# Second attention: turned 16-bit probability parts used as they are, and values kept as scaled pairs of 16-bit floats

## The chip, the cores and the metric

One core of a Trainium2 chip. The metric is the device time of one execution in microseconds (us). The engines that matter here: TensorE (PE; its weight loads are PEld), VectorE (DVE), ScalarE (ACT), GpSimd (POOL) and the queue of SyncE (SP), which issues the DMAs. Each engine runs its instructions in the order in which they stand on it.

## What is computed

A decoder of two layers over 512 positions of 1024 features. Layer 0 mixes with two block-sparse attentions, layer 1 with a "forgetting" attention (FoX) of 16 heads of 64; each layer ends in a squared-ReLU MLP. The change touches the second attention alone, `fox`:

```
q, k, v, fz = split(rmsnorm(h) @ w_in)
log_f = log_sigmoid(fz + b_forget);  cum = cumsum(log_f)
s = q.k * scale + cum[query] - cum[key];  p = softmax over keys <= query
o = p @ v;   h = h + concat(o) @ w_out
```

## The kernel before

All matrix products are made of pairs: a 32-bit operand is split into a high part (a rounding copy on ScalarE) and a low part (the operand less the high part, a subtraction on VectorE or GpSimd), and `mm3` adds three products, high·high, high·low and low·high. Weights come from DRAM in pieces of at most 128x1024 into a pool `raw` of five buffers; `split` issues the DMA and returns a function `parts`, which makes the pair in a pool `whl` of three. `load_cols` returns these functions and `cols` calls them at once. A string (`FOX_LOW`) says for each piece whether its low part is made by VectorE (D) or GpSimd (P).

`fox` runs as follows. `wv = self.cols(...)` loads and splits the first 272 columns of value and forget weights, in three pieces (3, 3 and 2 of the eight row blocks; 816, 816 and 544 columns). `norm_t` normalises the four row tiles of the residual stream, each in a buffer `xn` of the pool `raw` too: a Square with its sum on ScalarE, a chain of nine one-column operations on VectorE (`inv_rms`), a multiplication with the gain, eight transposes on TensorE, and again a pair, `xhi` (ScalarE) and `xlo` (VectorE). A string then orders the steps:

```
FOX_ORDER = "v0 f k0 k1 p0 k2 v1 p1 k3 p2 o01 k4 v2 p3 k5 p4 k6 v3 p5 k7 p6 o23 p7 o45 o67"
```

`v` are values of four heads (for each of four row tiles 24 matmuls into a PSUM bank `acc`, then a ScalarE copy and a VectorE subtraction into the pair `V[t]`), `f` the forget sums, which go through DRAM as extra rows of keys and queries, `k` queries and keys of two heads, `p` softmax and values of two heads, `o` the output projection.

For one head, `softmax_t` makes scores, exponentials and sums of four query tiles, scales the probabilities by 32768 over the sum and writes them as two 16-bit parts (`HL`: high by ScalarE, low by VectorE and GpSimd). One transposing DMA turns both into `HT`. One head later, `behind` takes them up: `turned` copies the turned high part to a 32-bit tile `PTh` on ScalarE and the turned low part to `PTl` on GpSimd; `pv` multiplies them with the value pair, eight matmuls of 512, 512, 384, 384, 128, 128, 256 and 256 columns; `combine` adds the halves and scales by 1/32768.

The instructions of all steps are put in order by a scheduler that works from its own model of durations, with `prio()` and `high_priority` ahead of the rest. Buffers are taken from their pool in that order: whatever needs a buffer stands behind what frees it.

Of the kernel before, what the change touches and what calls it, by code (L numbers as in the profile page):

```python
# [48 lines left out]
class Trunk:  # L49
# [28 lines left out]
    def split(self, srcs, shape, pool):  # L78


        nc = self.nc
        a, b = shape
        n = a * b
        raw = self.raw.tile([P, W_RAW], F32, tag="raw", name=self.nm("raw"))
        rv = raw[:, :n].rearrange("p (a b) -> p a b", a=a)
        for c0, c1, src in srcs:
            self.last_load = nc.sync.dma_start(rv[:, :, c0:c1], src)

        def parts():
            hl = (pool or self.whl).tile([P, 2, W_RAW], FR, tag="whl", name=self.nm("whl"))  # L90
            nc.scalar.activation(hl[:, 0, :n], raw[:, :n], AF.Copy)  # L91
            eng = nc.gpsimd if self.phase[self.pieces % len(self.phase)] == "P" else nc.vector
            self.pieces += 1
            eng.tensor_tensor(hl[:, 1, :n], raw[:, :n], hl[:, 0, :n].bitcast(F32), op=ALU.subtract)  # L94
            hv = hl[:, :, :n].rearrange("p t (a b) -> p t a b", a=a)
            return [(hv[:, 0, i], hv[:, 1, i]) for i in range(a)]
        return parts
# [310 lines left out]
    def softmax(self, passes, band, gate):  # L408

        nc = self.nc  # L410
        pt = self.pP.tile([P, PTW], F32, tag="P", name=self.nm("P"))
        st = self.sm.tile([P, 3, 4], F32, tag="sst", name=self.nm("sst"))
# [14 lines left out]
    def transpose_p(self, p):  # L427

        nc = self.nc
        hi = self.pPT.tile([P, PTW], FR, tag="PTh", name=self.nm("PTh"))  # L430
        lo = self.pPT.tile([P, PTW], FR, tag="PTl", name=self.nm("PTl"))
        for off, js in BANKS:
# [48 lines left out]
        nc.sync.dma_start_transpose(t, hl.rearrange("p a b -> p (a b)"))  # L481
        return t

    def turned(self, t):


        tv = t.rearrange("p (a b) c -> p a (b c)", a=2)
        hi = self.pPT.tile([P, PTW], FR, tag="PTh", name=self.nm("PTh"))
        lo = self.pPT.tile([P, PTW], FR, tag="PTl", name=self.nm("PTl"))
        with self.tc.issue_after(self.p_act.ins):  # L490
            self.nc.scalar.activation(hi, tv[:, 0], AF.Copy)
        with self.tc.issue_after(self.p_low.ins):
            self.round(lo, tv[:, 1])
        return hi, lo

    def pv(self, po, pt, vs, first, last):
        mm = self.nc.tensor.matmul
        js = [0, 1, 3, 2]
        for i, j in enumerate(js):
            w = S - j * P  # L500
            o = PTOFF[j]
            mm(po[:, j * P:], vs[j], pt[0][:, o:o + w], start=first and i == 0, stop=False)  # L502
            mm(po[:, j * P:], vs[j], pt[1][:, o:o + w], start=False, stop=last and i == 3)  # L503

    def combine(self, po, o, lower, scale=None):

        a, b = (slice(0, HD), slice(HD, P)) if lower else (slice(HD, P), slice(0, HD))
        if scale is None:
            self.nc.scalar.activation(o[a], po[b], AF.Copy)
            self.nc.vector.tensor_tensor(o[a], po[a], o[a], op=ALU.add)  # L510
        else:
            self.nc.scalar.activation(o[a], po[b], AF.Copy, scale=scale)
            self.nc.vector.scalar_tensor_tensor(o[a], po[a], scale, o[a], op0=ALU.mult, op1=ALU.add)

    def split_o(self, o):
        hl = self.pO.tile([P, 2, S], FR, tag="O", name=self.nm("O"))
# [668 lines left out]
    def fox(self, hs):  # L1185
        self.phase, self.pieces = FOX_LOW, 0
        nc, I = self.nc, self.I
        w = I["odd_w_in"][0]
        wo = I["odd_w_out"][0]
        lo, hi = slice(0, HD), slice(HD, P)  # L1190
        with ExitStack() as cx:
            pool = lambda name, bufs: cx.enter_context(self.tc.tile_pool(name=name, bufs=bufs))
            self.pP = pool("fP", 2)
            self.pPT = pool("fPT", 2)
            self.pHL = pool("fHL", 2)
            self.pHT = pool("fHT", 2)
            o2 = pool("fo", 2)
            a1 = cx.enter_context(self.tc.tile_pool(name="attf1", bufs=1))
            self.p_up = a1.tile([P, NT], F32, name="pup")
            nc.gpsimd.memset(self.p_up, P_UP)  # L1200
            wv = self.cols(w, [(2048, 2304), (3072, 3088)])
            x = self.norm_t(hs, self.row_tile(I["mix_norm"][1], "g"))
            zt = a1.tile([P, NT, 16], F32, name="zt")
            band = a1.tile([P, S], F32, name="mband")
            nc.gpsimd.memset(band, 0.0)
# [3 lines left out]
            pq = pool("fQ", 3)  # L1209
            self.pO = pool("fO", 4)  # L1210

            V = [a1.tile([P, 16, 2, HD], FR, tag=f"v{t}", name=f"v{t}") for t in range(NT)]

            def values(c):

                wc = wv if c == 0 else self.cols(w, [(2048 + 256 * c, 2304 + 256 * c)])
                for t in range(NT):
                    ps = self.psum("acc")
                    self.proj_n(ps, wc, 272 if c == 0 else 256, x, t)
                    if c == 0:  # L1220
                        nc.vector.tensor_copy(zt[:, t], ps[:, 256:272])
                    dst = V[t][:, 4 * c:4 * c + 4]
                    with self.tc.high_priority(offset=0):
                        pv = ps[:, :256].rearrange("p (h d) -> p h d", h=4)
                        nc.scalar.activation(dst[:, :, 0, :], pv, AF.Copy)
                        self.sub(dst[:, :, 1, :], pv, dst[:, :, 0, :])

            def forget():

                ft = lambda pool_, tag, name, dt: pool_.tile([P, PTW], dt, tag=tag, name=name)  # L1230
# [3 lines left out]
                for t in range(NT):  # L1234
# [10 lines left out]
                n, one = n1[:16, :S], n1[:16, S:2 * S]  # L1245
                nc.gpsimd.memset(one, 1.0)
                nc.vector.tensor_tensor_scan(n, one, e, 0.0, ALU.mult, ALU.add)
                rows = [ft(self.pPT, t_, f"frow{t_}", FR)[:16, :2 * S].rearrange("p (a b) -> p a b", a=2)
                        for t_ in ("PTh", "PTl")]
                nc.scalar.activation(rows[0][:, 0], n, AF.Copy)  # L1250
                nc.vector.tensor_tensor(rows[0][:, 1], n, rows[0][:, 0].bitcast(F32), op=ALU.subtract)
                nc.gpsimd.memset(rows[1][:, 0].bitcast(F32), -1.0)
# [32 lines left out]
            def behind():  # L1285

                head, t, ot = todo.pop()
                with self.prio():
                    pt = self.turned(t)
                    po = self.psum("o")  # L1290
                    self.pv(po, pt, [self.flat(V[t][:, head]) for t in range(NT)], True, True)
                    self.combine(po, ot, head % 2 == 0, 1.0 / P_UP)
                if head % 2:
                    o[head // 2] = self.split_o(ot)

# [10 lines left out]
            st, o = {}, {}  # L1306
# [59 lines left out]
```

## Time and profile before

| what | value |
|---|---|
| median of 3 runs | 1219.15 us (1218.03 to 1220.14) |
| the profiled execution's own time | 1223.81 us |
| its span, first to last instruction | 1222.1 us |
| mean granted TensorE clock | 0.991 of full speed |
| TensorE busy | 1196.8 us (98%) |
| weight loads / VectorE / ScalarE / GpSimd busy | 1011.4 / 966.5 / 679.3 / 501.9 us |

Times within the execution are in us from the span's start; the second attention lies between about 640 and 873. In a row of the order in time stand start, duration, engine, line and operation, output<-inputs, and in brackets the idle time of the engine just before, with what ended it. Matmuls are pipelined, so the step from one start to the next tells their pace, not the duration. In a row of groups stand line, engine, operation, tiles and shapes, count, busy us and mean ns of one, then the idle us before them. A row of stretches is explained where it is shown.

### The profile page before, as it was taken

To read this page: it belongs to the slowest core of one execution; us is meant where nothing else is said; L and a number is where in the kernel's file an instruction comes from. 1 tells how busy PE (TensorE), PEld (TensorE's weight loads), DVE (VectorE), ACT (ScalarE), POOL (GpSimd) and SP (SyncE) were. 2 spreads that over 40 slices of the span, in tenths; PEclk is the share of its full clock that TensorE was granted. 3 is DMA by queue.
4 is the path that set the end of the run, shared out by engine and by line. 5 is a ranking of instruction groups with operands and counts; after the bars stand their busy time and mean duration, and the time that the engine had idled before them with its cause. 6 is when DMAs were issued, how large, how long until landed. Compare 5 with 4: busy or idle time off the path is not lost.

```text
span 1222.1 us, 16954 instructions
## 1 busy us (share of the span) xinstructions
PE 1196.8 (98%) x6055; PEld 1011.4 (83%) x6055; DVE 966.5 (79%) x1619; ACT 679.3 (56%) x1243; POOL 501.9 (41%) x503
## 2 busy tenths in 40 slices
PE   9989999999999999999999999999999999999997
PEld 7779987887988888888888888888888888888886
DVE  6868778887878977898877677577787798779875
ACT  6446756784654554455425876687555445544542
POOL 3424555563352333233102665566354323432314
PEclk9989999999999999999999989999999999999999
DMA  8952242131543243324105565554563323332201
GB/s 241 333 147 79 68 119 76 51 106 41 150 122 92 87 122 105 101 87 134 40 2 148 131 137 129 122 106 118 158 167 111 106 87 104 108 111 91 87 1 69
DMA packets 183440, 134.25 MB, mean 110 GB/s; under 512 B 47875, under 2 KB 158635, under 8 KB 183356
## 3 DMA queue, kind: packets, MB, share of 16 engines
q1 hardware_dynamic: 183196, 132.94, 38.7%
q8 instruction: 48, 0.79, 0.3%
q14 instruction: 36, 0.29, 0.1%
q10 hardware_dynamic: 160, 0.23, 0.1%
HBM read 120.27 MB, written 7.64 MB: 105 GB/s over the span
## 4 chain that ended last, share of the span: by engine, by line
PE 68%; DVE 3%; ACT 2%; issue 1%; DMA 1%; POOL 0%; DVEq 0%; ACTq 0%; POOLq 0%
PE acc L129 13%; PE acc L131 13%; PE acc L130 13%; PE s L1126 13%; PE o L1126 6%; PE pt L1126 3%; PE s L130 1%; PE s L131 1%; PE s L129 1%; PE o L503 1%; PE o L502 1%; PE s L456 1%; PE o L131 1%; PE o L130 1%; PE o L129 1%
## 5 line engine op out<-in xcount | busy, mean ns | idle before, releaser
L131 PE MATMUL acc<-xhi,whl 128*128 128x512 f32 (+1 forms) x768 | 295.6, 385 | 3.6 <-DVE whl L94 2.5
L129 PE MATMUL acc<-xhi,whl 128*128 128x512 f32 (+1 forms) x768 | 294.6, 384 | 0.7 <-DVE Q L402 0.4
L130 PE MATMUL acc<-xlo,whl 128*128 128x512 f32 (+1 forms) x768 | 293.8, 383 | 0.0
L94 DVE TENSOR_TENSOR whl<-raw,whl 128x1024 fp32r<-128x1024 f32 (+2 forms) x110 | 164.2, 1497 | 82.2 <-ACT whl L91 73.6
L1029 POOL TENSOR_TENSOR r<-r,yrow 128x512 f32<-128x512 f32 x64 | 98.2, 1534 | 317.6 <-ACT r L1028 316.3
L91 ACT ACTIVATE whl<-raw 128x1024 fp32r<-128x1024 f32 (+1 forms) x139 | 144.7, 1047 | 51.0 <-PE acc L131 33.4
L131 PEld LDWEIGHTS acc<-xhi,whl 128*128 128x128 f32 x768 | 145.2, 189 | 33.0 <-DVE whl L94 4.0
L129 PEld LDWEIGHTS acc<-xhi,whl 128*128 128x128 f32 x768 | 145.1, 189 | 28.5 <-PE acc L131 0.8
L1126 PE MATMUL s<-whl,sp 128*128 128x512 f32 x672 | 167.6, 390 | 0.0
L130 PEld LDWEIGHTS acc<-xlo,whl 128*128 128x128 f32 x768 | 145.2, 189 | 26.8
L1126 PEld LDWEIGHTS s<-whl,sp 128*128 128x128 f32 x672 | 126.2, 188 | 26.6
L1080 ACT ACTIVATE whl<-w 128x1024 fp32r<-128x1024 f32 x98 | 103.6, 1059 | 71.3 <-PE s L1126 43.7
L1081 DVE TENSOR_TENSOR whl<-w,whl 128x1024 fp32r<-128x1024 f32 x98 | 135.0, 1379 | 8.5 <-ACT whl L1080 8.5
L1028 ACT ACTIVATE r<-acc 128x512 f32<-128x512 f32 x62 | 37.1, 598 | 117.1 <-PE acc L131 117.1
L94 POOL TENSOR_TENSOR whl<-raw,whl 128x1024 fp32r<-128x1024 f32 x29 | 71.5, 2469 | 50.9 <-ACT whl L91 49.7
L1126 PE MATMUL o<-whl,sp 128*128 128x512 f32 x336 | 88.8, 391 | 0.0
L1086 DVE TENSOR_TENSOR w<-w,w 128x1024 f32<-128x1024 f32 x56 | 82.0, 1464 | 0.9
L1134 DVE TENSOR_TENSOR x<-s,x 128x512 f32<-128x512 f32 x112 | 74.9, 680 | 3.0 <-PE s L1126 3.0
L1126 PEld LDWEIGHTS o<-whl,sp 128*128 128x128 f32 x336 | 63.3, 188 | 13.6
L400 DVE TENSOR_TENSOR sp<-act,sp 128x512 fp32r<-128x512 f32 x64 | 69.5, 1108 | 0.6 <-ACT sp L1037 0.6
L1031 ACT ACTIVATE act<-r 128x512 f32<-128x512 f32 x64 | 40.4, 633 | 45.7 <-POOL r L1029 45.6
L422 ACT ACTIVATE P<-P,sst 128x128 f32<-128x128 f32 (+1 forms) x96 | 53.3, 557 | 14.4 <-DVE sst L421 12.6
(297 smaller groups left out, 2503.1 us busy)
## 6 DMA issues: line engine op xcount, KB each, us to landing
raw<-in_mlp_w SPq DMA_DIRECT2D x72, 512.0 KB
w<-in_mlp_w SPq DMA_DIRECT2D x56, 512.0 KB
raw<-in_odd_w_in SPq DMA_DIRECT2D x22, 512.0 KB
raw<-in_even_w_in SPq DMA_DIRECT2D x20, 512.0 KB
band<-bias_dram SPq DMA_DIRECT2D x24, 256.0 KB
bias_dram<-bias_rows SPq DMA_DIRECT2D x16, 320.0 KB
raw<-in_even_w_out SPq DMA_DIRECT2D x8, 512.0 KB
raw<-in_odd_w_out SPq DMA_DIRECT2D x8, 512.0 KB
```

Source lines behind the costliest of these rows:

```text
L91: nc.scalar.activation(hl[:, 0, :n], raw[:, :n], AF.Copy)
L94: eng.tensor_tensor(hl[:, 1, :n], raw[:, :n], hl[:, 0, :n].bitcast(F32), op=ALU.subtract)
L129: mm(ps, ahl[0], bhl[0], start=first, stop=False)
L130: mm(ps, ahl[0], bhl[1], start=False, stop=False)
L131: mm(ps, ahl[1], bhl[0], start=False, stop=last)
L400: self.nc.vector.tensor_tensor(out, ps, hi.bitcast(F32), op=ALU.subtract)
L1029: nc.gpsimd.tensor_tensor(r, r, row, op=ALU.mult)
L1080: nc.scalar.activation(t[:, 0], src, AF.Copy)
L1081: nc.vector.tensor_tensor(t[:, 1], src, t[:, 0].bitcast(F32), op=ALU.subtract)
L1086: nc.vector.tensor_tensor(out, a_, b_, op=op)
L1126: mm = lambda l, r, first, last: nc.tensor.matmul(ps, l, r, start=first, stop=last, skip_group_check=True)
L1134: nc.vector.tensor_tensor(hv, ps, hv, op=ALU.add)
```

## The change

The turned 16-bit parts go to TensorE as they are: `turned` with its two copies is gone, and so are the tiles `PTh` and `PTl` of `fox`. The values, the other operand, are therefore kept as 16-bit pairs. So that they fit, the values of each four heads are multiplied by one number `y`, which bounds them: `bound_gain` takes the largest gain once, `value_scale` adds up the squares of the weights used (made by a second ScalarE pass in `parts`, whose output goes to the place of the low part and is overwritten by it), sums them over partitions with a matmul against ones, and makes `y` and its inverse in seven small VectorE operations. `combine` multiplies by the inverse. The first three pieces are now loaded at the start, but split in `values(0)`, which stands behind `norm_t`. The first value matmul of a head also waits for the last ScalarE copy of the newest `HL`. `P` and `HT` have three buffers instead of two, the forget rows tiles of their own.

```
-        def parts():
+        def parts(squares=None):
             hl = (pool or self.whl).tile([P, 2, W_RAW], FR, tag="whl", name=self.nm("whl"))
             nc.scalar.activation(hl[:, 0, :n], raw[:, :n], AF.Copy)
+            if squares is not None:
+                c, out = squares
+                scratch = hl[:, 1, :n].rearrange("p (a b) -> p a b", a=a)
+                nc.scalar.activation(scratch[:, :, :c], rv[:, :, :c], AF.Square, accum_out=out)
...
-    def turned(self, t):
...
-            self.nc.scalar.activation(hi, tv[:, 0], AF.Copy)
...
-            self.round(lo, tv[:, 1])
...
+    def bound_gain(self, g, out):
+        v = self.nc.vector
+        v.tensor_reduce(out, g, axis=AX.X, op=ALU.max, apply_absolute_value=True)
+        v.tensor_scalar(out, out, 1e-12, None, op0=ALU.max)
+        v.reciprocal(out, out)
+        v.tensor_scalar(out, out, 0.9 * V_UP / 32, None, op0=ALU.mult)
+    def value_scale(self, squares, gain, out):
+        nc = self.nc
+        n = squares.shape[1]
+        ps = self.psum("acc")
+        nc.tensor.matmul(ps[:, :n], self.ones, squares, start=True, stop=True)
+        y, u = out[:, 0:1], out[:, 1:2]
+        nc.vector.tensor_reduce(u, ps[:, :n], axis=AX.X, op=ALU.add)
+        nc.vector.tensor_scalar(y.bitcast(I32), u.bitcast(I32), 1, None, op0=ALU.logical_shift_right)
+        nc.vector.tensor_scalar(y.bitcast(I32), y.bitcast(I32), -1, 0x5F3759DF, op0=ALU.mult, op1=ALU.add)
+        nc.vector.tensor_tensor(y, y, gain, op=ALU.mult)
+        nc.vector.reciprocal(u, y)
+        nc.vector.tensor_scalar(u, u, 1.0 / P_UP, None, op0=ALU.mult)
...
-            wv = self.cols(w, [(2048, 2304), (3072, 3088)])
-            x = self.norm_t(hs, self.row_tile(I["mix_norm"][1], "g"))
+            wv = self.load_cols(w, [(2048, 2304), (3072, 3088)])
+            g = self.row_tile(I["mix_norm"][1], "g")
+            vgain = a1.tile([P, 1], F32, name="vgain")
+            self.bound_gain(g, vgain)
+            x = self.norm_t(hs, g)
...
-            V = [a1.tile([P, 16, 2, HD], FR, tag=f"v{t}", name=f"v{t}") for t in range(NT)]
+            V = [a1.tile([P, 16, 2, HD], F16, tag=f"v{t}", name=f"v{t}") for t in range(NT)]
...
-                wc = wv if c == 0 else self.cols(w, [(2048 + 256 * c, 2304 + 256 * c)])
+                calls = wv if c == 0 else self.load_cols(w, [(2048 + 256 * c, 2304 + 256 * c)])
+                wc = [pair for i, call in enumerate(calls) for pair in call((256, vsq[:, c, i:i + 1]))]
+                self.value_scale(vsq[:, c, :len(calls)], vgain, vscale[:, c])
+                y = vscale[:, c, 0:1]
...
-                        nc.scalar.activation(dst[:, :, 0, :], pv, AF.Copy)
-                        self.sub(dst[:, :, 1, :], pv, dst[:, :, 0, :])
+                        nc.scalar.activation(dst[:, :, 0, :], pv, AF.Copy, scale=y)
+                        nc.vector.scalar_tensor_tensor(dst[:, :, 1, :], pv, y, dst[:, :, 0, :], op0=ALU.mult, op1=ALU.subtract)
...
-                    pt = self.turned(t)
                     po = self.psum("o")
-                    self.pv(po, pt, [self.flat(V[t][:, head]) for t in range(NT)], True, True)
-                    self.combine(po, ot, head % 2 == 0, 1.0 / P_UP)
+                    self.pv(po, (tv[:, 0], tv[:, 1]), [self.flat(V[t][:, head]) for t in range(NT)], True, True, self.p_act)
+                    self.combine(po, ot, head % 2 == 0, vscale[:, head // 4, 1:2])
```

The lines of the changed kernel have other numbers than before: 94 became 99, 160 became 165, 202 became 207, 388 and 393 became 393 and 398, 1173 became 1198, and 129 to 131 became 134 to 136.

At the start of the second attention, on VectorE. `x3` is the residual stream's last row tile, to which the MLP's last sums are added; `whl_955` to `whl_957` are the first three pieces of value weights, `nrm` the chains of the row tiles' norms, `xn` the normalised row tiles. Before, from the MLP's last two additions on:

```order
L1173 TENSOR_TENSOR x3_126<-s_931_6108,x3_126 128x512
L166 TENSOR_SCALAR nrm_951_6243<-nrm_951_6243 128x1
L168 TENSOR_SCALAR nrm_951_6243<-nrm_951_6243 128x1
L169 TENSOR_SCALAR nrm_951_6243<-nrm_951_6243 128x1
L168 TENSOR_SCALAR nrm_951_6243<-nrm_951_6243 128x1
L169 TENSOR_SCALAR nrm_951_6243<-nrm_951_6243 128x1
L1173 TENSOR_TENSOR x3_126<-o_932_6122,x3_126 128x512
L168 TENSOR_SCALAR nrm_951_6243<-nrm_951_6243 128x1
L169 TENSOR_SCALAR nrm_951_6243<-nrm_951_6243 128x1
L393 TENSOR_TENSOR xlo_941_6185<-pt_944_6200,xhi_940_6184 128x4x128
L202 SCALAR_TENSOR_TENSOR xn_950_6242<-x2_124,nrm_951_6243,g_939_6182 128x512 x2
```

The same place now:

```order
L1198 TENSOR_TENSOR x3_126<-s_931_6108,x3_126 128x512
L1198 TENSOR_TENSOR x3_126<-o_932_6122,x3_126 128x512
L493 TENSOR_REDUCE vgain_6172<-g_936_6170 128x1
L99 TENSOR_TENSOR whl_955_6310<-raw_933_6161,whl_955_6310 128x816
L99 TENSOR_TENSOR whl_956_6314<-raw_934_6164,whl_956_6314 128x816
L494 TENSOR_SCALAR vgain_6172<-vgain_6172 128x1
L99 TENSOR_TENSOR whl_957_6318<-raw_935_6167,whl_957_6318 128x544
L506 TENSOR_REDUCE vscale_6292<-acc_958_6322 128x1
L398 TENSOR_TENSOR xlo_938_6178<-pt_941_6193,xhi_937_6177 128x4x128
L398 TENSOR_TENSOR xlo_938_6178<-pt_942_6200,xhi_937_6177 128x4x128
```

The low parts of the three pieces stood far ahead of this place and now stand between the MLP's last addition and the first low part of `x`; the chains of row tiles 1 to 3, which ran between the additions, all stand behind these rows.

On ScalarE at the same place. `act`'s last work is over; `raw_933` to `raw_935` are the three pieces. Before:

```order
L91 ACTIVATE whl_922_6016<-raw_921_6014 128x1024
L160 ACTIVATE xn_942_6186,nrm_943_6187<-x0_107 128x1024
L160 ACTIVATE xn_946_6214,nrm_947_6215<-x1_116 128x1024
L160 ACTIVATE xn_950_6242,nrm_951_6243<-x2_124 128x1024
L392 ACTIVATE xhi_940_6184<-pt_944_6200 128x4x128
L160 ACTIVATE xn_954_6270,nrm_955_6271<-x3_126 128x1024
L392 ACTIVATE xhi_940_6184<-pt_945_6207 128x4x128
```

Now:

```order
L92 ACTIVATE whl_922_6016<-raw_921_6014 128x1024
L165 ACTIVATE xn_939_6179,nrm_940_6180<-x0_107 128x1024
L96 ACTIVATE whl_955_6310,vsq_6291<-raw_933_6161 128x3x256
L96 ACTIVATE whl_956_6314,vsq_6291<-raw_934_6164 128x3x256
L96 ACTIVATE whl_957_6318,vsq_6291<-raw_935_6167 128x2x256
L397 ACTIVATE xhi_937_6177<-pt_941_6193 128x4x128
L397 ACTIVATE xhi_937_6177<-pt_942_6200 128x4x128
L165 ACTIVATE xn_943_6207,nrm_944_6208<-x1_116 128x1024
L165 ACTIVATE xn_947_6235,nrm_948_6236<-x2_124 128x1024
L165 ACTIVATE xn_951_6263,nrm_952_6264<-x3_126 128x1024
```

The Squares of the value weights came in, and the norm's own Squares of row tiles 1 to 3 moved behind the high part of row tile 0.

On TensorE in the step `v1`, at the value matmuls of the second head (those into `o`, from `V[0]` = `v0` and so on). Before, they stand behind the first 24 matmuls of the new values:

```order
L129 MATMUL acc_1029_6812<-whl_1028_6809,xhi_940_6184 128x256
L130 MATMUL acc_1029_6812<-whl_1028_6809,xhi_940_6184 128x256
L131 MATMUL acc_1029_6812<-whl_1028_6809,xlo_941_6185 128x256
L502 MATMUL o_1044_6964<-PTh_1042_6960,v0_6311 128x512
L503 MATMUL o_1044_6964<-PTl_1043_6961,v0_6311 128x512
L502 MATMUL o_1044_6964<-PTh_1042_6960,v1_6312 128x384
L503 MATMUL o_1044_6964<-PTl_1043_6961,v1_6312 128x384
```

Now:

```order
L135 MATMUL acc_1015_6764<-xlo_938_6178,whl_1014_6761 128x512
L136 MATMUL acc_1015_6764<-xhi_937_6177,whl_1014_6761 128x512
L504 MATMUL acc_1028_6825<-vsq_6291,ones_83 128x2
L517 LDWEIGHTS v0_6306
L517 MATMUL o_1042_6981<-HT_1008_6716,v0_6306 128x512
L517 LDWEIGHTS v0_6306
L517 MATMUL o_1042_6981<-HT_1008_6716,v0_6306 128x512
L517 LDWEIGHTS v1_6307
L517 MATMUL o_1042_6981<-HT_1008_6716,v1_6307 128x384
```

They moved ahead of the new values' 24, straight behind the keys of step `k2`, read `HT` itself, and have weight loads of their own; the sum of the squares stands ahead of them.

More of the change, by code (lines that the diff above doesn't have):

```diff
@@ L28 @@
 P_UP = 32768.0
+V_UP = 32768.0
 PTW = 1280
@@ L482, in softmax_t, with pv, mm @@
         return t
-    def turned(self, t):
[L487 to L492, printed above, removed]
-            self.round(lo, tv[:, 1])
-        return hi, lo
-    def pv(self, po, pt, vs, first, last):
-        mm = self.nc.tensor.matmul
+    def bound_gain(self, g, out):
[16 more added lines that the diff above has]
+        nc.vector.tensor_scalar(u, u, 1.0 / P_UP, None, op0=ALU.mult)
+    def pv(self, po, pt, vs, first, last, after=None):
+        def mm(*args, **kw):
+            nonlocal after
+            i = self.nc.tensor.matmul(*args, **kw)
+            if after is not None:
+                self.tc.add_manual_dep(i.ins, after.ins.name, mybir.DependencyInfo(
+                    mybir.DependencyClass.Sync, mybir.DependencyReason.DATA), reason="turned by then")
+                after = None
         js = [0, 1, 3, 2]
@@ L511, in combine @@
         else:
-            self.nc.scalar.activation(o[a], po[b], AF.Copy, scale=scale)
-            self.nc.vector.scalar_tensor_tensor(o[a], po[a], scale, o[a], op0=ALU.mult, op1=ALU.add)
+            self.nc.scalar.activation(o[a], po[b], AF.Copy, scale=scale[b])
+            self.nc.vector.scalar_tensor_tensor(o[a], po[a], scale[a], o[a], op0=ALU.mult, op1=ALU.add)
     def split_o(self, o):
@@ L1192, in fox @@
             pool = lambda name, bufs: cx.enter_context(self.tc.tile_pool(name=name, bufs=bufs))
-            self.pP = pool("fP", 2)
-            self.pPT = pool("fPT", 2)
+            self.pP = pool("fP", 3)
             self.pHL = pool("fHL", 2)
-            self.pHT = pool("fHT", 2)
+            self.pHT = pool("fHT", 3)
             o2 = pool("fo", 2)
@@ L1200, in fox @@
             nc.gpsimd.memset(self.p_up, P_UP)
-            wv = self.cols(w, [(2048, 2304), (3072, 3088)])
-            x = self.norm_t(hs, self.row_tile(I["mix_norm"][1], "g"))
+            wv = self.load_cols(w, [(2048, 2304), (3072, 3088)])
[3 more added lines that the diff above has]
+            x = self.norm_t(hs, g)
+            vsq = a1.tile([P, 4, 3], F32, name="vsq")
+            vscale = a1.tile([P, 4, 2], F32, name="vscale")
             zt = a1.tile([P, NT, 16], F32, name="zt")
@@ L1247, in forget @@
                 nc.vector.tensor_tensor_scan(n, one, e, 0.0, ALU.mult, ALU.add)
-                rows = [ft(self.pPT, t_, f"frow{t_}", FR)[:16, :2 * S].rearrange("p (a b) -> p a b", a=2)
-                        for t_ in ("PTh", "PTl")]
+                rows = [a1.tile([16, 2, S], FR, name=f"frow{i}") for i in range(2)]
                 nc.scalar.activation(rows[0][:, 0], n, AF.Copy)
@@ L1287, in behind @@
                 head, t, ot = todo.pop()
+                tv = t.rearrange("p (a b) c -> p a (b c)", a=2)
                 with self.prio():
-                    pt = self.turned(t)
                     po = self.psum("o")
-                    self.pv(po, pt, [self.flat(V[t][:, head]) for t in range(NT)], True, True)
-                    self.combine(po, ot, head % 2 == 0, 1.0 / P_UP)
+                    self.pv(po, (tv[:, 0], tv[:, 1]), [self.flat(V[t][:, head]) for t in range(NT)], True, True, self.p_act)
+                    self.combine(po, ot, head % 2 == 0, vscale[:, head // 4, 1:2])
                 if head % 2:
```

## The prediction

> **What bounds the kernel now.** I read the page first (busy shares, the chain that ended last), then busy time in stretches of the second attention, then the order in time of single engines at its start and at its two gaps. Rows of the stretches: us, then busy us (and instructions) of TensorE, its weight loads, VectorE, ScalarE and GpSimd, the granted TensorE clock, DMA share, GB/s.
>
> ```profile
> PE 1196.8 (98%) x6055; PEld 1011.4 (83%) x6055; DVE 966.5 (79%) x1619; ACT 679.3 (56%) x1243; POOL 501.9 (41%) x503
> PE 68%; DVE 3%; ACT 2%; issue 1%; DMA 1%; POOL 0%; DVEq 0%; ACTq 0%; POOLq 0%
> 640.46:657.30 16.84, 16.38 (x133) 15.84 (x132) 11.81 (x31) 8.35 (x15) 2.59 (x6) 1.00 0.60 164
> 660.00:700.00 40.00, 39.56 (x193) 33.27 (x192) 27.21 (x64) 30.27 (x64) 21.68 (x26) 1.00 0.53 134
> 720.00:800.00 80.00, 79.94 (x425) 68.67 (x424) 53.87 (x108) 54.07 (x115) 45.31 (x50) 1.00 0.57 133
> 820.00:870.00 50.00, 49.44 (x238) 40.22 (x236) 34.33 (x68) 32.08 (x64) 33.55 (x32) 1.00 0.62 138
> 702.50:707.00 4.50, 1.71 (x10) 1.27 (x9) 3.11 (x5) 3.71 (x9) 3.23 (x3) 0.85 0.78 149
> 707.00:712.40 5.40, 5.38 (x25) 5.38 (x26) 5.27 (x13) 4.99 (x14) 3.17 (x5) 0.50 0.38 103
> 808.30:811.30 3.00, 1.22 (x9) 1.04 (x8) 2.91 (x12) 2.95 (x8) 2.10 (x4) 1.00 0.90 166
> 811.30:815.20 3.90, 3.90 (x21) 3.88 (x20) 3.75 (x6) 3.06 (x9) 3.13 (x4) 0.56 0.28 108
> ```
>
> TensorE is the bound: it works 79.94 of 80 us between 720 and 800. ScalarE and GpSimd, whose work the change removes, have room there, so that work is worth something only at two places: 702.5 to 712.4 and 808.3 to 815.2, where TensorE first waits and then runs at about half clock. These are what a lighter ScalarE and GpSimd can give back:
>
> ```profile
> 704.00 0.50 PE L456 MATMUL s<-K,Q 128*128 128x512 f32 x1 [1.28 <-POOL K L406]
> 707.02 0.58 PE L129 MATMUL acc<-whl,xhi 128*128 128x256 f32 x1 [1.53 <-DVE v L400]
> 810.31 0.36 PE L129 MATMUL acc<-whl,xhi 128*128 128x256 f32 x1 [1.78 <-DVE K L400]
> ```
>
> Ceiling: waits of 1.28+1.53+1.78 = 4.6 us, and clock losses of 5.4 x 0.50 = 2.7 and 3.9 x 0.44 = 1.7: 9.0 us.
>
> **The change, part by part.**
>
> *Conversions removed.* 16 ScalarE copies and 16 GpSimd copies of the turned parts, one of each for a head. With them, the copy that the weights' split makes, and one turning by DMA:
>
> ```profile
> L91 ACT ACTIVATE whl<-raw 128x1024 fp32r<-128x1024 f32 x30 | 31.1, 1048 | 1.8 <-PE acc L131 1.8
> L491 ACT ACTIVATE PTh<-HT 128x1280 fp32r<-128x1280 f16 x16 | 20.2, 1265 | 10.9 <-DMA HT<-HL 10.9
> L406 POOL TENSOR_SCALAR PTl<-HT 128x1280 fp32r<-128x1280 f16 x16 | 20.5, 1284 | 10.2 <-DMA HT<-HL 9.2 <-PE acc L131 1.0
> 694.67 3.06 SPq L481 DMA_TRANSPOSE HT<-HL  x1
> 699.71 1.27 ACT L491 ACTIVATE PTh<-HT 128x1280 fp32r<-128x1280 f16 x1 [0.32 <-DMA HT<-HL]
> ```
>
> *Work added on ScalarE and others.* Nine Squares over the value weights: six of 1024 columns, three of 768, 768 and 512. They are not in the trace; the split's copy of the same columns took 1.05, so 6.3+2.1 = 8.4 us, three of them before the attention. So ScalarE gains 20.2-8.4 = 11.8 us over some 230, but at the two gaps, which lie in the stages that make values, it loses two Squares and gains three copies: 3.8-2.1 = 1.7 us each. VectorE gets 24 small operations more for the scales and four for the gain, some 0.15 us each. Four matmuls of two or three columns on TensorE: nothing at best, a 128-column transpose's pace at worst (eight in 1.03 us, below), which I take: +0.4. The scaled value copies and the scaled last sum replace instructions of the same shape, and the forget rows' own tiles only take a wait off GpSimd: nothing. No DMA is added or dropped. The first value matmul of a head now also waits for the last ScalarE copy of the next head's parts; that copy is queued before the transpose lands, so it costs nothing while the transpose is the later one.
>
> *The value matmuls on TensorE.* Eight a head, 2560 columns together, now 16-bit with 128 explicit weight loads. Before, a block of eight in a row, and the 256-column matmul ahead of it:
>
> ```profile
> 701.17 0.28 PE L131 MATMUL acc<-whl,xlo 128*128 128x256 f32 x1
> 701.29 0.40 PE L502 MATMUL o<-PTh,v 128*128 128x512 f32 x1
> 701.52 0.40 PE L503 MATMUL o<-PTl,v 128*128 128x512 f32 x1
> 702.45 0.28 PE L503 MATMUL o<-PTl,v 128*128 128x256 f32 x1
> L503 PEld LDWEIGHTS o<-PTl,v 128*128 128x128 f32 x64 | 12.1, 189 | 1.2
> ```
>
> From 701.29 to 702.45, and 0.12 for the last (the pace of 256 columns, 701.17 to 701.29): 1.28 us. No 16-bit matmul stands in the trace. Its bounds: at the pace of the 512-column ones (701.29 to 701.52, 0.23) 2560 columns take 1.15, so -0.13 x 16 = -2.1 us; on the other side every explicit load uncovered, 128 x 0.189 = +24. I exclude most of that, since 1011 us of weight loads already lie under 1197 us of matmuls, and take half the gain: -1.1. [...]
>
> *The start of the second attention: what moves.* The first three pieces of value weights were split during the MLP. Now only the ScalarE copies stay there; the VectorE halves (816, 816, 544 columns) stand behind the MLP's last residual add, and behind the new maximum of the gain. Until they have run, their raw buffers stay taken; the pool has five (three pieces, the gain, row tile 0), so the normalised row tiles 1 to 3 have none, and their Squares and chains come after. Rows of before, with the replay in this order:
>
> ```profile
> 621.80 1.23 DVE L94 TENSOR_TENSOR whl<-raw,whl 128x1024 fp32r<-128x1024 f32 x1 [0.40 <-ACT whl L91]
> 640.46 1.03 PE L388 MATMUL pt<-ident,xn 128*128 128x128 f32 x8
> 640.66 0.69 DVE L1173 TENSOR_TENSOR x<-o,x 128x512 f32<-128x512 f32 x1 [0.16 <-PE o L131]
> 641.73 0.69 DVE L393 TENSOR_TENSOR xlo<-pt,xhi 128x512 fp32r<-128x512 f32 x1
> 641.75 0.39 PE L129 MATMUL acc<-whl,xhi 128*128 128x272 f32 x1 [0.25 <-ACT xhi L392]
> 642.33 1.40 DVE L202 SCALAR_TENSOR_TENSOR xn<-x,nrm,g 128x512 f32<-128x512 f32 x2
> L168 DVE TENSOR_SCALAR nrm<-nrm 128x1 f32<-128x1 f32 x12 | 3.2, 270 | 0.3
> L169 DVE TENSOR_SCALAR nrm<-nrm 128x1 f32<-128x1 f32 x12 | 2.6, 213 | 0.3
> L162 DVE TENSOR_SCALAR nrm<-nrm 128x1 f32<-128x1 f32 x4 | 0.6, 152 | 0.5 <-ACT xn L160 0.3
> 656.90 0.29 PE L130 MATMUL acc<-whl,xhi 128*128 128x272 f32 x1
> 657.03 0.29 PE L131 MATMUL acc<-whl,xlo 128*128 128x272 f32 x1
> ```
>
> The add ends at 641.35. The maximum over 1024 columns is not in the trace: between the 0.69 of 512 columns and twice the 1024-column subtraction; I take that row, 1.23: 642.6. The three halves, 2176 columns at 1.23/1024: 2.6, so 645.2; two small operations, 645.5; the two low halves of row tile 0, 646.2 and 646.9. TensorE's third value matmul needs the first of them: it stands from about 641.5 to 646.2, where before it ran on from 641.75. Then VectorE does 31 small operations: three chains of 3 x 0.15 + 3 x (0.27+0.21) = 1.9, less the 0.7 that come later, and seven of the scales, together 6.0 by durations, of which neighbours overlap (642.33 starts before 641.73+0.69 is out): 4 to 6, taken 5: 651.9. Row tile 1 is multiplied by 653.3, tile 2 by 654.7; a copy and two small ones, 655.2; the low half of tile 1, 655.9. From there TensorE is paced by itself and VectorE: 22 matmuls at 0.125 and four transposes, 659.1; tile 2 from 659.8 to 663.0; tile 3 to 666.3. Before, the last one started at 657.03 and ended its share by 657.15. So 9 us later. Nothing covers it: k0's projections stand behind these matmuls on TensorE, and the forget rows, which the first scores need, behind tile 3.
>
> The clock makes it worse. Above, 2.8 us of waiting within 4.5 cost half clock for 5.4 us, and 1.78 within 3.0 did for 3.9. The 4.7 us gap does so surely: tile 0's 24 matmuls at the 5.4/25 = 0.216 of those rows take 5.2 instead of 3.0 us, to 651.4, which the wait for tile 1 (to 652.6) hides. The second gap, some 2.3 us of waiting between 652 and 655.9, can halve it again for tile 1's 22: up to 22 x 0.09 = +2.0; I take +1. In all +10; bounds 6 (a fast maximum, chains overlapping fully) and 13. [...]
>
> *The gaps.* Around 700 the new order puts the second head's value matmuls ahead of the first 24 of the next values, 24 x 0.12 = 2.9 us earlier, at 698.4 in the old scale. Its transpose was issued at 694.67 and landed by 699.7. In the new ScalarE order two Squares (2.1) and no copy (1.2) stand ahead of its last parts, while GpSimd loses the 1.27 ahead of its own: about 0.5 later, 700.2. So TensorE waits 1.8 there for the DMA, a new wait in place of the old two, with the next values and two heads' scores queued behind it, and some 0.5 later on, less dense than 2.8 in 4.5; the clock drop may go. I take 3 of 5.5 back there, and 1 of 3.5 at the other place: -4.0; bounds 0 and -9.0.
>
> **Sum**, against the profiled execution's 1223.81 us: +10.0 +0.4 -1.1 -4.0 = +5.3. The median shown is 4.66 lower (0.4%), so 1219.15+5.3 = 1224.5.
>
> **Rivals.** *The attention gives back more than the start takes* (faster). Place: the two gaps; if the freed ScalarE and GpSimd close them wholly, 9.0+2.1, the start would have to cost under 8.3 to end 2.4 below: with 7 for it, 1219.15+7.4-11.1 = 1215.5. For it: both are waits behind ScalarE, GpSimd and VectorE. Against: the Squares fall just there, and the transpose's 5 us stay. *They cancel* (within 0.2%, 2.4 us, which is about what a measurement of this kernel can tell): gains 7.5 to 11 against 10: about 1219.5. *Explicit loads show*: if a fifth of 128 x 0.189 is uncovered, +4.8 in place of -1.1: 1230; for it only that the form is unseen. *The conversions did not matter and nothing else does*: the start's cost alone, no gap returned, +9.3: 1228.5, part of the forecast's upper side.
>
> **Chances.** The forecast (+2.4 to +9.5) 0.54; cancelled 0.24; faster 0.13; loads uncovered or longer half clock (above +9.5) 0.09. Slower by over 0.2%: 0.54+0.09 = 0.63. The forecast's own range is 1221.5 to 1228.6; with the cases on both sides, 1215.5 to 1231.
>
> **What would show it.** Right: between 640 and 667 TensorE idle for 8 us or more instead of 1.3, released by the low halves of xlo and by xn; granted clock well under 1 there; the last value matmul of the first piece near 666; 16 x 1.1 to 1.3 us for value matmuls; a wait for the transpose near the old 700. Wrong: the clock at 1.00 in 640 to 660 and no wait over 2 us there, or the stretch from 667 on shorter than before's 657 on by more than 8 us.

## The result, and the profile after

The changed kernel takes 1227.96 us (median of 6 runs, 1226.38 to 1230.57), the kernel before in the same measurements 1219.12 us: +8.8 us, ratio 1.0069 with a 95% interval of 1.0049 to 1.0089. It is slower, as forecast, and 3.5 us above the forecast number.

The two profiled executions don't differ by 8.8 in a simple way. Before the second attention, where TensorE's work is the same in both programs, the one of before lost some 6 us early in the run. Busy time in the stretch 50 to 100, of before and then of after (us, busy us and instructions of TensorE, its weight loads, VectorE, ScalarE and GpSimd, granted clock, DMA share, GB/s):

```profile
50.00:100.00 50.00, 45.84 (x228) 38.29 (x227) 36.35 (x58) 23.19 (x42) 21.00 (x28) 0.93 0.62 192
```
```profile
50.00:100.00 50.00, 48.75 (x267) 41.73 (x266) 38.68 (x73) 27.11 (x51) 24.89 (x29) 1.00 0.66 194
```

So I compare lengths from the MLP's end on. The first transposition after the MLP starts at 640.46 in before and at 634.29 in after; the first one after the attention, in TensorE's order in time, at 873.07 and at 878.03:

```profile
873.07 1.03 PE L388 MATMUL pt<-ident,xn 128*128 128x128 f32 x8
```
```profile
634.29 1.03 PE L393 MATMUL pt<-ident,xn 128*128 128x128 f32 x8
878.03 1.03 PE L393 MATMUL pt<-ident,xn 128*128 128x128 f32 x8
```

The second attention takes 243.74 us instead of 232.61, +11.1. What follows it is as long as before (348.97 us to the end of the span, 349.03 in before).

**Its start in after**, TensorE's, VectorE's and ScalarE's order in time:

```profile
634.49 0.85 ACT L96 ACTIVATE whl<-raw 128x768 fp32r<-128x768 f32 x1 [11.21 <-PE o L136]
636.16 0.61 ACT L96 ACTIVATE whl<-raw 128x512 fp32r<-128x512 f32 x1
635.10 1.21 DVE L493 TENSOR_REDUCE vgain<-g 128x1 f32<-128x1024 f32 x1
636.23 2.12 DVE L99 TENSOR_TENSOR whl<-raw,whl 128x816 fp32r<-128x816 f32 x2
638.34 0.71 DVE L99 TENSOR_TENSOR whl<-raw,whl 128x544 fp32r<-128x544 f32 x1
636.92 0.38 PE L504 MATMUL acc<-vsq,ones 128*128 128x3 f32 x2 [1.59 <-ACT whl L96]
639.77 0.60 PE L136 MATMUL acc<-whl,xlo 128*128 128x272 f32 x1 [1.85 <-DVE xlo L398]
657.94 0.29 PE L136 MATMUL acc<-whl,xlo 128*128 128x272 f32 x1
```

TensorE waits twice: 1.59 us for the third Square, because the sums' matmul stands ahead of the value matmuls, and 1.85 us for the low half of row tile 0, behind the maximum and the three low halves on VectorE. The last value matmul of this piece starts 23.65 us after the MLP's end (657.94-634.29), against 16.57 before (657.03-640.46): +7.1. The first row names what held it up: ScalarE, idle for 11.21 us, starts its Squares only when the MLP's last matmul (PE o) is done, although the weights are there (the same Square runs at 582.50 in scale_tiles_early, below).

**Later waits in after**, TensorE's order in time, with the sums' matmul of the second piece and VectorE's reading of it:

```profile
700.18 0.28 PE L504 MATMUL acc<-vsq,ones 128*128 128x2 f32 x2
701.80 1.25 PE L517 MATMUL o<-HT,v 128*128 128x512 f16 x8 [1.35 <-ACT P L466]
703.43 0.14 DVE L506 TENSOR_REDUCE vscale<-acc 128x1 f32<-128x2 f32 x1
703.63 0.38 PE L134 MATMUL acc<-whl,xhi 128*128 128x256 f32 x1 [0.58 <-DVE vscale L506]
708.93 1.25 PE L517 MATMUL o<-HT,v 128*128 128x512 f16 x8 [0.91 <-ACT v L1257]
712.01 0.38 PE L461 MATMUL s<-K,Q 128*128 128x256 f32 x1 [0.84 <-DVE sst L465]
814.60 0.76 PE L461 MATMUL s<-K,Q 128*128 128x512 f32 x2 [1.32 <-POOL K L411]
857.60 1.25 PE L517 MATMUL o<-HT,v 128*128 128x512 f16 x8 [0.60 <-DMA HT<-HL]
862.20 1.26 PE L517 MATMUL o<-HT,v 128*128 128x512 f16 x8 [1.52 <-DMA HT<-HL]
```

The two gaps of before (at 704 and at 810) have not closed, and at the end the last two heads' value matmuls wait for their turning. Busy time of after in stretches shows the clock:

```profile
634.29:657.94 23.65, 19.18 (x132) 18.13 (x131) 19.04 (x61) 12.80 (x25) 2.67 (x6) 0.86 0.45 118
640.20:644.70 4.50, 4.50 (x22) 4.50 (x22) 4.50 (x34) 0.74 (x2) 0.00 (x0) 0.51 0.42 115
698.50:714.17 15.67, 11.29 (x66) 8.85 (x66) 14.54 (x39) 13.32 (x34) 11.08 (x14) 0.96 0.80 165
714.17:719.70 5.53, 5.53 (x28) 5.53 (x28) 3.78 (x15) 3.65 (x12) 2.07 (x4) 0.50 0.40 76
814.60:819.00 4.40, 4.40 (x22) 4.29 (x23) 4.37 (x14) 3.79 (x13) 2.12 (x3) 0.61 0.04 17
856.00:865.00 9.00, 6.87 (x36) 4.67 (x36) 6.02 (x8) 2.75 (x4) 5.57 (x3) 1.00 0.84 202
```

A new half-clock stretch at the start, and one still at each gap. In 698.5 to 714.2 VectorE works 14.54 of 15.67 us and ScalarE 13.32: there VectorE has next to no room for anything added.

### The profile page after: what moved, and what is told of

It is laid out like the page before. It is cut to its first block, busy times and chain, and to the rows that moved or that the text cites. A ratio compares the mean times of both kernels' runs of the same rounds, so it can differ in the third digit from the quotient of the medians.

```text
span 1227.0 us, 16988 instructions
## 1 busy us (share of the span) xinstructions
PE 1196.1 (97%) x6063; PEld 1004.3 (82%) x6063; DVE 964.3 (79%) x1647; ACT 673.3 (55%) x1245; POOL 479.5 (39%) x487
## 5 line engine op out<-in xcount | busy, mean ns | idle before, releaser
L99 DVE TENSOR_TENSOR whl<-raw,whl 128x1024 fp32r<-128x1024 f32 (+1 forms) x110 | 162.5, 1482 | 80.2 <-ACT whl L92 70.5
L92 ACT ACTIVATE whl<-raw 128x1024 fp32r<-128x1024 f32 x139 | 144.7, 1048 | 51.5 <-PE acc L136 36.6
```

## The experiments

Times are medians, with the ratio to the kernel before timed beside them; the last column is the second attention by the first transpositions after the MLP and after the attention, as above. The kernel before took 1218.5 to 1220.5 us in the sittings of these runs, so kernels of different sittings are compared by their ratios.

| kernel | us | ratio (95%) | attention, us |
|---|---|---|---|
| before | 1219.1 | 1 | 232.61 |
| after | 1228.0 | 1.0069 (1.0049 to 1.0089) | 243.74 |
| scale_tiles_early | 1221.3 | 1.0015 (1.0000 to 1.0031) | 233.34 |
| plain16 | 1213.6 | 0.9951 (0.9932 to 0.9970) | 227.41 |
| pv16_copies | 1226.7 | 1.0055 (1.0036 to 1.0074) | 240.87 |
| no_copy_wait | 1225.4 | 1.0052 (1.0031 to 1.0072) | 240.13 |
| squares_only | 1217.0 | 0.9973 (0.9959 to 0.9987) | 229.06 |
| chain_only | 1219.1 | 0.9995 (0.9980 to 1.0009) | 233.12 |
| own_scratch | 1217.4 | 0.9983 (0.9968 to 0.9997) | 231.45 |
| dead_copies | 1225.2 | 1.0049 (1.0027 to 1.0070) | 239.06 |
| sums_in_o | 1216.1 | 0.9980 (0.9963 to 0.9996) | 229.78 |
| sums_in_s | 1214.6 | 0.9958 (0.9942 to 0.9974) | 228.10 |

**scale_tiles_early: what holds the start.**

```
-            vgain = a1.tile([P, 1], F32, name="vgain")
+            vgain = self.const.tile([P, 1], F32, name="vgain")
...
-            vsq = a1.tile([P, 4, 3], F32, name="vsq")
-            vscale = a1.tile([P, 4, 2], F32, name="vscale")
+            vsq = self.const.tile([P, 4, 3], F32, name="vsq")
+            vscale = self.const.tile([P, 4, 2], F32, name="vscale")
```

> The changed kernel with one thing altered: the three small tiles of the value scale (column sums, gain, scale) lie in the permanent pool instead of the second attention's new pool. Theory M (memory): the new pool takes over memory that the MLP's tiles hold until its last matmul, so the Squares write their sums only then, and the low halves, which overwrite the Squares' scratch, come after them; with the tiles elsewhere Squares, maximum and low halves go back into the MLP, the stretch from the MLP's end to the last value matmul of the first piece shrinks from 24.4 us to 17 to 18.5, and the time falls by 6 to 7 to 1221 to 1222. Rival C (code order): the call that makes the low halves stands behind the normalisation, as my prediction had it; then nothing moves: 1228, stretch 24.

Measured 1221.3, -6.7 against after. ScalarE's and TensorE's order in time, and busy time, in this kernel:

```profile
582.50 0.84 ACT L96 ACTIVATE whl<-raw 128x768 fp32r<-128x768 f32 x1
595.90 0.62 ACT L96 ACTIVATE whl<-raw 128x512 fp32r<-128x512 f32 x1
635.71 1.03 PE L393 MATMUL pt<-ident,xn 128*128 128x128 f32 x8
652.28 0.29 PE L136 MATMUL acc<-whl,xlo 128*128 128x272 f32 x1
```
```profile
635.71:652.30 16.59, 16.13 (x131) 15.62 (x130) 12.18 (x31) 8.37 (x15) 2.69 (x6) 1.00 0.60 167
```

The first Square runs at 582.50, 53 us ahead of the MLP's end, and the start takes 16.57 us (652.28-635.71), the very length of before, at full clock. (The expectation counts 24.4 us for this stretch in after; by the rows shown here it is 23.65.) The calls stand where they stood. So theory M holds and rival C, the code order, is excluded: three tiles of 84 bytes a partition together, put into memory that the MLP still used, cost 7 us. (The attention is 10.4 shorter than in after; the 3.3 beyond the start lie between two profiles with the same order of work there, and the medians show 6.7 in all.)

**plain16: the change without its scale.** The value weights are split at their load, and the scale is a constant:

```
...
-                wc = [pair for i, call in enumerate(calls) for pair in call((256, vsq[:, c, i:i + 1]))]
-                self.value_scale(vsq[:, c, :len(calls)], vgain, vscale[:, c])
-                y = vscale[:, c, 0:1]
+                wc = wv if c == 0 else self.cols(w, [(2048 + 256 * c, 2304 + 256 * c)])
+                y = 64.0
...
-                    self.combine(po, ot, head % 2 == 0, vscale[:, head // 4, 1:2])
+                    self.combine(po, ot, head % 2 == 0, 1.0 / (64.0 * P_UP))
```

> The changed kernel with a constant 64 as value scale: no Squares, no gain maximum, no column sums, no scale chain, value weights split at their load as before; 16-bit value matmuls without conversions stay. The scale that guards against overflow is left out. Theory S: the waits of the changed kernel in the stages that make values come from the Squares and the scale chain; then what stays is the gain of the value matmuls (-2.9) and of the lighter engines (0 to -4): 1212 to 1216.5. Rival P: they come from the value matmuls' earlier place in TensorE's queue, where the DMA turning has not landed; then the stages still lose 3 to 5: 1219 to 1222.

1213.6: theory S. This kernel is an experiment only, since it leaves out the guard against overflow. It is 7.7 us below scale_tiles_early, which differs from it by the scale alone, and 5.9 below the kernel before timed beside it. TensorE's longest wait left is one of 1.84 us near the old 704, in TensorE's order in time:

```profile
701.19 0.35 PE L134 MATMUL acc<-whl,xhi 128*128 128x256 f32 x1 [1.84 <-DVE K L405]
```

**pv16_copies: 16-bit value matmuls alone**, in the kernel before (with the constant scale of 64, and tiles of their own for the forget rows).

```
-        hi = self.pPT.tile([P, PTW], FR, tag="PTh", name=self.nm("PTh"))
-        lo = self.pPT.tile([P, PTW], FR, tag="PTl", name=self.nm("PTl"))
+        hi = self.pPT.tile([P, PTW], F16, tag="PTh", name=self.nm("PTh"))
+        lo = self.pPT.tile([P, PTW], F16, tag="PTl", name=self.nm("PTl"))
...
-            V = [a1.tile([P, 16, 2, HD], FR, tag=f"v{t}", name=f"v{t}") for t in range(NT)]
+            V = [a1.tile([P, 16, 2, HD], F16, tag=f"v{t}", name=f"v{t}") for t in range(NT)]
```

> The kernel before with the value matmuls alone in 16 bit: the copies of the turned parts stay, as 16-bit to 16-bit copies, and values are stored as 16-bit pairs with a constant scale of 64; no Squares, no scale chain. By the trace of the changed kernel (a block of eight takes 1.10 us of TensorE's time against 1.28) -2.9: 1216.2. By the term of my prediction -1.1: 1218. If explicit weight loads showed, at or above 1219.

A miss on all three counts: 1226.7. The matmuls did what the first line expects. One block of eight, first and last row, and then what cost more, TensorE's, VectorE's and GpSimd's order in time:

```profile
863.25 0.39 PE L502 MATMUL o<-PTh,v 128*128 128x512 f16 x1
864.13 0.27 PE L502 MATMUL o<-PTh,v 128*128 128x256 f16 x1
864.24 0.27 PE L503 MATMUL o<-PTl,v 128*128 128x256 f16 x1
847.26 3.38 DVE L94 TENSOR_TENSOR whl<-raw,whl 128x1024 fp32r<-128x1024 f32 x1
850.70 0.50 PE L130 MATMUL acc<-whl,O 128*128 128x512 f32 x1 [2.42 <-DVE whl L94]
864.83 2.65 POOL L94 TENSOR_TENSOR whl<-raw,whl 128x1024 fp32r<-128x1024 f32 x1 [4.79 <-ACT whl L91]
867.45 0.62 POOL L406 TENSOR_SCALAR O<-o 128x512 fp32r<-128x512 f32 x1
868.13 0.50 PE L129 MATMUL acc<-whl,O 128*128 128x512 f32 x1 [2.21 <-POOL O L406]
```

A block takes 863.25 to 864.24 and 0.11 for the last (864.13 to 864.24): 1.10 us against 1.28. But the scheduler set another order on GpSimd (in before this rounding stands ahead of that low half, at 865.38 and 868.16), and at the end of the attention TensorE waits 2.42 us for a low half of output weights and 2.21 us for the last pair's rounding, queued on GpSimd behind such a half. Waits of that size stand nowhere in before's end. The kernel therefore doesn't isolate the matmuls' worth in time; it shows that an edit can lose more through the order it leads to than it gains.

**no_copy_wait: the added dependency.**

```
-                    self.pv(po, (tv[:, 0], tv[:, 1]), [...], True, True, self.p_act)
+                    self.pv(po, (tv[:, 0], tv[:, 1]), [...], True, True)
```

> The changed kernel without the added dependency of a head's first value matmul on the newest ScalarE copy of the next head. If the 1.35 us wait at 701.8 is that dependency, it goes, with up to 1.3 us of the time: 1226.5 to 1227. If TensorE waits there for the landing of the transpose, which came at the same moment, the wait stays and the time is 1228.

1225.4, below both numbers expected; the intervals of this ratio and of after's overlap, so a gain is not shown. The wait is still there, and the profile now names the transpose:

```profile
702.92 1.25 PE L517 MATMUL o<-HT,v 128*128 128x512 f16 x8 [2.54 <-DMA HT<-HL]
```

By this row of TensorE's order in time the transpose is what comes last. The block starts 67.6 us after the first transposition (702.92-635.33), in after 67.5 (701.80-634.29): without the added dependency it starts no earlier.

**squares_only and chain_only: which part of the scale.** Both start from scale_tiles_early. The first keeps the Squares and sets `y = 64.0`; the second keeps the chain, shortens the Squares to one column in 256 and lowers the scale 16-fold to match:

```
-                wc = [pair for i, call in enumerate(calls) for pair in call((256, vsq[:, c, i:i + 1]))]
+                wc = [pair for i, call in enumerate(calls) for pair in call((1, vsq[:, c, i:i + 1]))]
```

> The kernel of scale_tiles_early with the Squares kept but their sums unread: the value scale is a constant 64, without gain maximum, column sums and scale chain. Between plain16 (1213.6) and scale_tiles_early (1221.3) lie 7.7 us. Theory A: the nine Squares cost them (ScalarE time, and the low halves queued behind them): 1219 to 1221. Theory B: the chain from column sums to scale costs them: 1213.5 to 1216.

> The kernel of scale_tiles_early with the whole chain from column sums to scale, but the Squares taken over one column in 256 (the bound then rests on those columns alone, with the scale lowered 16-fold). Theory A (the Squares' ScalarE time): 1213.5 to 1216. Theory B (the chain: the sums' matmul keeps one of two accumulator banks until VectorE comes to it, and the value copies wait for the scale): 1219 to 1221. If each has a share, both this and squares_only land between 1216 and 1219.

1217.0 and 1219.1. By ratios the chain costs 0.0044 over plain16 (5.4 us; 5.7 of the attention's length), beyond the intervals; the Squares 0.0022 (2.7 us; 1.65 of its length), which the intervals don't separate from nothing. So theory B carries most of it, and theory A alone is excluded. TensorE's order in time in chain_only:

```profile
696.12 0.39 PE L134 MATMUL acc<-whl,xhi 128*128 128x256 f32 x1 [1.21 <-DVE vscale L506]
705.80 0.55 PE L134 MATMUL acc<-whl,xhi 128*128 128x256 f32 x1 [4.14 <-DVE K L405]
```

The sums' matmul takes one of the two accumulator banks, and TensorE's next value matmul waits until VectorE, in its own order, has read it: that is the first wait. The second is for the low half of K. The chain itself was over long before (its last operation there ends at 697.68). VectorE's order in time in chain_only, two rows, and K's low half in plain16:

```profile
698.45 3.28 DVE L484 SCALAR_TENSOR_TENSOR HL<-P,sst,HL 128x384 f16<-128x384 f32 x2 [0.77 <-POOL K L411]
704.97 0.69 DVE L405 TENSOR_TENSOR K<-acc,K 64x512 fp32r<-64x512 f32 x1
```
```profile
700.35 0.69 DVE L405 TENSOR_TENSOR K<-acc,K 64x512 fp32r<-64x512 f32 x1
```

In chain_only K's low half stands behind these parts of `HL`, a head's last sum and the next head's scores; in plain16 the last sum (701.08) and the `HL` part (701.80) come after it. By these rows this wait comes from the order that the scheduler set around the chain, not from the chain's own time. How the 5.4 us divide between the bank and the order, no run shows.

**own_scratch, sums_in_o, sums_in_s: mending it.** In own_scratch the Squares of the later pieces get a scratch tile and stand behind the low half; in the other two also the bank of the sums is changed:

```
             eng.tensor_tensor(hl[:, 1, :n], raw[:, :n], hl[:, 0, :n].bitcast(F32), op=ALU.subtract)
+            if squares is not None and squares[2] is not None:
+                c, out, sqs = squares
+                scratch = sqs[:, :a * c].rearrange("p (a b) -> p a b", a=a)
+                nc.scalar.activation(scratch, rv[:, :, :c], AF.Square, accum_out=out)
...
-        ps = self.psum("acc")
+        ps = self.psum("s")
```

(The last two lines are those of sums_in_s; sums_in_o has `"o"` there.)

> The kernel of scale_tiles_early with the Squares of the three later pieces of value weights written to a scratch tile of their own, behind the low halves instead of ahead of them. By theory A the low halves come 1 us earlier for each piece, and the time falls by 1 to 3, to 1218.5 to 1220.5. By theory B the scale only comes later: 1221 to 1223.

> The kernel of own_scratch with the column sums' matmul in one of the two PSUM banks of the value outputs (o) instead of the accumulator banks of the projections (acc). In own_scratch TensorE waits 2.6 us in three places for the scale chain's reading of that bank. If the bank is the cost, these waits go and the time falls by 2 to 4, to 1213.5 to 1215.5. If the scale itself is late for the value copies, or the o bank is as scarce, it stays within 1 of 1217.4.

> As sums_in_o, with the sums in one of the two banks of the scores (s). Same two expectations: 1213.5 to 1215.5 if the shared accumulator bank is the cost, within 1 of 1217.4 if not; above 1218.5 if the scores then wait for their bank.

1217.4, 1216.1 and 1214.6. own_scratch fell further than either theory had said, and its interval lies below that of scale_tiles_early: the place of the Squares and low halves matters too, so theory A had a share. sums_in_o missed: by ratio it is no faster than own_scratch (0.9980 and 0.9983), and TensorE waits 1.84 us for K's low half at 701.63. With the sums in a score bank, too, the scale's reading no longer holds TensorE: the wait of own_scratch at 696.46 is gone, and the longest one left is 1.53 us, at full clock (TensorE's order in time of own_scratch, then of sums_in_s; the clock is shown in the last section):

```profile
696.46 0.38 PE L138 MATMUL acc<-whl,xhi 128*128 128x256 f32 x1 [1.22 <-DVE vscale L510]
```
```profile
702.74 0.38 PE L138 MATMUL acc<-whl,xhi 128*128 128x256 f32 x1 [1.53 <-DVE v L1263]
```

sums_in_s keeps the whole scale and is faster than before (0.9958) and than after; its interval separates it neither from plain16, without the scale, nor quite from own_scratch (0.9974 and 0.9968 are the ends that overlap). So the wait for the bank is shown, and that it goes; what the bank alone costs in time is not.

**dead_copies: what the removed copies are worth.**

```
+                    for tag, half, after, op in (("PTh", 0, self.p_act, lambda d, s: nc.scalar.activation(d, s, AF.Copy)),
+                                                 ("PTl", 1, self.p_low, self.round)):
+                        dead = self.pPT.tile([P, PTW], F16, tag=tag, name=self.nm(tag))
+                        with self.tc.issue_after(after.ins):
+                            op(dead, tv[:, half])
```

> The kernel of plain16 with the 16 ScalarE and 16 GpSimd copies of the turned parts put back into tiles that nothing reads; TensorE still takes the turned parts themselves. If the relief of ScalarE and GpSimd carries part of plain16's gain (5.9 us, of which 3.1 is the pace of the 16-bit value matmuls), the time rises by 1.5 to 3.5, to 1215 to 1217; if only the missing step between turning and matmul does, it stays at 1213.6.

1225.2: 11.6 us above plain16, far over the 1.5 to 3.5 expected. Busy time at the first of the two places, in dead_copies and in plain16:

```profile
694.00:706.00 12.00, 7.92 (x42) 5.77 (x40) 10.70 (x21) 11.30 (x26) 10.68 (x12) 0.73 0.62 145
```
```profile
694.00:706.00 12.00, 9.69 (x61) 7.77 (x59) 10.39 (x24) 8.81 (x24) 8.64 (x11) 0.86 0.51 117
```

With the copies ScalarE works 11.30 of 12 us and GpSimd 10.68, without them 8.81 and 8.64: there the copies fill the two engines that make K's parts, for which TensorE waits 5.0 us in two places of this kernel (2.30 at 698.72 and 2.68 at 806.14), and at the first its clock is 0.73 against 0.86. (For the pace of the value matmuls the runs give 2.9, 16 x 0.18, where the expectation has 3.1.) How much of the 11.6 is the copies' own time and how much the order that the scheduler set around them, this run does not part.

## Why the prediction was right

The sign and the range were right, and so was the start as a loss, in the main for the reasons given. That the sum came within 3.5 us is partly luck: the start was forecast 2.9 too dear and the value matmuls' gain 1.8 too small, which offset part of an error of 8.7 in the gaps. With that error alone the time would have been about 1233 (1224.5+8.7), outside the range.

**The start, forecast +10 (6 to 13): measured +7.1.** Right are the work behind the MLP's last add, the maximum's price (1.23 taken, 1.21 measured), the wait for row tile 0's low half, and half clock for its matmuls (0.51 over 4.5 us). Idle is 4.5 (23.65-19.18), not 8 or more, and the last value matmul, at 657.94, is at 664.1 on before's scale, where the first transposition is 6.17 later, not near 666. The step that failed is the second gap: the 31 small operations, taken at 5 us, ran in 3.3 (640.23 to 643.51), beside the matmuls at half clock, so tile 1 came in time. Two things were not in it: the sums' matmul waiting for the Squares (1.59), and why the low halves moved. The prediction took their new place from the order; the reading behind it, the later call (rival C above), was wrong. It is the memory of the scale's three tiles, as scale_tiles_early shows, which moves all three at once. That the raw buffers held the row tiles back was not tried apart.

**The value matmuls, forecast -1.1: measured -2.9** (16 x 0.18; -2.7 by a block of before whose next matmul follows at once, 729.11 to 730.38, 1.27). This lies beyond the end of -2.1 that I had set from the 512-column pace of the 32-bit form. Two things were mis-sized: half the gain was held back for loads that might show, and in after none does (TensorE's 4.3 us of idle time before L517 ended with a DMA, 2.1, or with ScalarE, 1.3 and 0.9); and the 16-bit matmuls have a faster pace here, 1.10 against the 1.15 of that bound. By line, TensorE's weight loads of after:

```profile
L517 PEld LDWEIGHTS <-v x128: 95/98/181, 695.9 to 863.1; 128*128 128x128 f16 x128
```

98 ns in the median, against a mean of 189 for the 32-bit loads of L503 in before. A bound had from the 32-bit form did not hold for this one.

**The gaps, forecast -4.0: measured about +4.7.** This is the term that failed. Without the scale the kernel does give back there: plain16's -5.9 less the matmuls' -2.9 leaves -3.0. But I priced the scale by busy time only: the Squares went against the copies that fall away (a net relief of 1.7 us of ScalarE at each gap), the "24 small operations" (six for each four heads, L506 to L511) came into the sum at nothing there, and the sums' matmuls at +0.4, which no run measures apart; scale_tiles_early less plain16 puts the scale at +7.7. What was missing is what stands behind it: the bank that the sums hold (waits of 1.21 and 0.77 us in chain_only), and the order that the scheduler sets on a VectorE with next to no room. (The prediction's 11.8 us of relief on ScalarE subtracts all nine Squares, although it puts three of them ahead of the attention; no term rests on it.)

**The wait for the transpose near the old 700** came as forecast (1.35 forecast as 1.8), and two more at the end (0.60, 1.52) that I had not looked for.

So +7.1 -2.9 +4.7 = +8.9, against +8.8. That this closes proves little, since the gaps' term is itself had from differences of medians. By the two profiles alone, whose attentions are 11.1 apart, the gaps would be at +6.9 (11.1-7.1+2.9); single executions differ (those of scale_tiles_early lie between 1217.7 and 1225.0). The rival "nothing returned" gave 1228.5 and has the number, but not the way: a good deal was returned, and the scale took it.

## What to carry to other kernels

A tile in a newly opened pool inherits the memory of the phase before (7 us here, by scale_tiles_early): ask what still uses it, since whatever writes the tile, and all that is queued behind, waits for that; the same few bytes in a permanent pool cost nothing that was measured here. Price a small chain not by its durations but by what it holds meanwhile (a PSUM bank, for which TensorE waited 1.21 us in chain_only, or a place in a full engine's queue), by who is next, and by the order that the scheduler will set around it. And price a removed operation at its place, by how full its engine is there (ScalarE 11.30 of 12 us in dead_copies), not over the span.

## What the runs showed of the hardware

**The clock after waits.** At the start of after, with waits of 1.59 (to 636.92) and 1.85 us (to 639.77), the clock was 0.50 from 637.80 to 644.63; behind the one of 1.78 in before (to 810.31) it was 0.56 over 811.30 to 815.20. A lone wait's length didn't decide it in these runs: the one of 1.32 in after, at 814.60, left 0.61 over the next 4.4 us, while those of 1.35 in after and 1.53 in sums_in_s left it at 1.00 over the next 4.0. In the traces of before and after the clock changes only at edges that lie a multiple of 3.41 us apart: it is 0.50 in 67.37 to 74.20, 705.67 to 712.49 and 811.48 to 814.89 of before, and in 637.80 to 644.63, 712.90 to 719.72 and 815.30 to 818.71 of after. Busy time in two such slices of after, then in two stretches of the same length of sums_in_s:

```profile
811.89:815.30 3.41, 2.09 (x13) 1.73 (x13) 3.21 (x9) 1.62 (x4) 1.96 (x4) 1.00 0.83 220
815.30:818.71 3.41, 3.41 (x18) 3.41 (x17) 3.38 (x12) 2.83 (x9) 1.45 (x3) 0.50 0.00 0
```
```profile
698.43:701.84 3.41, 2.40 (x16) 1.67 (x13) 2.12 (x4) 3.36 (x8) 3.06 (x3) 1.00 0.00 0
701.84:705.25 3.41, 2.51 (x21) 2.51 (x22) 3.32 (x12) 3.13 (x8) 2.48 (x5) 1.00 0.46 103
```

The wait of 1.32 lies within one slice, which is busy for 2.09 of 3.41 us (0.61), and the next slice has half clock. The wait of 1.53, from 701.21 to 702.74, is spread over both stretches shown, which are busy for 0.70 and 0.74, and the clock stays at 1.00. Before and after have 672 slices at full clock between 20 and 1190 us: the three with a busy share up to 0.51 were followed by half clock, three of five between 0.55 and 0.61, and none of the others, all from 0.68 on.

**VectorE beside GpSimd.** One step of the chain, on one column, took 2.29 us, where the median of its four runs is 0.15, while GpSimd made a low half (VectorE's and GpSimd's order in time in after):

```profile
809.68 2.29 DVE L509 TENSOR_TENSOR vscale<-vscale,vgain 128x1 f32<-128x1 f32 x1
809.55 2.40 POOL L99 TENSOR_TENSOR whl<-raw,whl 128x1024 fp32r<-128x1024 f32 x1 [0.31 <-ACT whl L92]
```

It ends as GpSimd's does (811.97 and 811.95). A low half on VectorE at 65.16 in before took 3.33 us, against a median of 1.23 (L94), while GpSimd made one from 65.04 to 67.41. No run here took the GpSimd instruction away, so what lengthened them was not shown.
